# Three side works of a fused attention trunk, moved in its issue order: weight sums, two heads' decay, gate rows

## The chip, the cores and the metric

One core of a Trainium2 chip runs the program. The metric is the device time of one execution in microseconds. A matmul engine (PE, with its weight loads PEld), a vector engine (DVE), a scalar engine (ACT), GpSimd (POOL) and a queue that issues transfers (SP) each work through their own rows in order and meet in semaphores.

## The reference

One layer over 1024 tokens of width 1024. A normalised, modulated input h goes through one wide projection. Its parts feed two gated recurrences, HGRN2 (eight heads) and GLA (four heads), which run chunk by chunk, and their results are projected, gated, merged and projected once more.

```
mod = c_act @ ada_w + ada_b;  shift, scale, gate = split(mod, 3)
h = rms_norm(x, norm_w) * (1 + scale) + shift
hq, hf, hi, hz, gq, gk, gv, gz, ga, mg = split(h @ w_in, IN_OFFSETS)
y_h = hgrn2_branch(hq, hf, hi, hz, ...)                # S_t = diag(f_t) S + k_t v_t^T, o = S^T q
log_a = log_sigmoid(ga @ alpha_w + alpha_b) / 16       # the GLA decay, per head
y_g = gla_branch(gq, gk, gv, gz, log_a, ...)
merged = sigmoid(mg0) * (y_h @ w_branch0) + sigmoid(mg1) * (y_g @ w_branch1)
x = x + gate * (merged @ w_out);  return rms_norm(x, final_norm_w)
```

## The kernel before

**Arithmetic.** Every float32 factor is split in a high part (a cast on ACT, L211) and a low part (a subtraction on DVE, L212), and three matmuls make one product. The large products are cut in 2 x 2 blocks and done as seven block products instead of eight (numbers 1, 2, 5, 3, 6, 7, 4, in this order). Products 5, 3, 6 and 7 need sums of weight blocks, and 5, 6, 7 and 4 need an activation factor of their own.

**Stages.** PE does in turn: a first stage; V0, the GLA values (`Vstage(0)`, L2002); gate and key features of GLA (L607); V1, the HGRN values (`Vstage(1)`, L2002 again); F (`Fstage(2)`), features of HGRN heads; the remaining features (L607); the last stages (L1422) and the output. In the profile V0 runs from 110 to 194 us, the GLA features to 285, V1 to about 375 and F to about 467.

**The stream.** `Stream.go` (L843 on) takes job by job. After every unit, six matmuls or about 1.4 us of PE, it calls `weave`, which steps three tracks: `side` (the attention heads), `more` and `back`. An entry of a track is a generator, a countdown, a rate and the unit from which it may start; only the first entry of a track is stepped, and a generator yields how many units it wants to pass. V0 takes units 0 to 56, the GLA features 56 to 104, V1 104 to 160, F 160 to 216. Before each job, `ahead` loads jobs in advance and prepares (casts and splits) at most the next one, if the pool of 46 slots has room:

```
room = lambda: len(S.free_list)
...
d = self.prepped - i
if d > preps or d > 0 and room() < job.parts + 1:
    break
job.prep()
```

`parts` is 2 for products 1, 2 and 3, whose activation factor lies ready, and 4 for the others. A job that wasn't prepared ahead is prepared when its turn comes. A slot is 128 x 1024 float32; the free slot that was given back first is taken first.

**The side work that the change touches.** `v_sums(s)` (L1819) makes the weight sums of V1 (s = 1) and of F (s = 2). For each half kk it loads four weight blocks (L1829, on SP), makes four sums on DVE (L1832, L1834, L1836, L1838) and stores them from POOL (L1840). `alpha_side((2, 3))` (L932) makes the decay of GLA heads 2 and 3: matmuls (L389), ACT L943 to L960 with several table loads, DVE L949, L950 and L957. `gate_side` (L1086) sums the rows of the gate's modulation on DVE (L1099, L1101). `prepare` (L1280) makes the weight sums of the last stages, with at least 11 free slots, and is held from the start of V1 to near the end of F by `pause`.

**The heads.** `attention` (L639) works a head: ACT L657 and DVE L658 to L661 make a first factor xb from q and the decay, PE scores it (L665), DVE L667 to L670 and L684 scale q and k; DVE L693 and L694 make the next xb for PE L698; DVE L726 and L727 go before PE L767 and L791; DVE L771 and ACT L779 and L795 copy the scores, ACT L792 copies k for PE L815, and DVE L819 and L821 make the state for PE L834 and L836. L1054 loads q and k, L1006 the values; L1019, L1024 and L1030 collect the head's result, and PE L992 and L993, ACT L994 and L995 and DVE L1038 norm it. GLA head 0 runs beside the end of V0 and the first features, head 1 beside the last features, head 2 beside V1. L1888 is DVE's eviction of V0, L1860 ACT's copies out of the accumulator.

The built program has a fixed order of rows on each engine, made by a scheduler from the order in which the code issues them and their dependences, with some rows (`held`) kept in the program's order. Lines behind L1842 are two less in the changed kernel, and the four sums are L1831, L1833, L1835 and L1837 there.

Of the kernel before, what the change touches and what calls it, by code (L numbers as in the profile page):

```python
# [14 lines left out]
ALU = mybir.AluOpType  # L15
# [74 lines left out]
def hybrid_trunk_kernel(  # L90
# [6 lines left out]
    nc = tc.nc  # L97
# [9 lines left out]
    S = Slots(sp, N_SLOTS)  # L107
# [7 lines left out]
    def mtile():  # L115
        cnt[0] += 1
        return ps_m.tile([P, 512], F32, tag="m", name=f"pm{cnt[0]}")
# [79 lines left out]
    def split(src, hi=None, lo=None):  # L197

        if hi is None:
            hi = S.get(list(src.shape[1:]), F32R)  # L200
            lo = S.get(list(src.shape[1:]), F32R)
        nc.scalar.copy(hi, src)  # L202
        nc.vector.tensor_sub(lo, src, hi.bitcast(F32))  # L203
        return hi, lo

    held = tc.keep_in_program_order
# [180 lines left out]
    def mm_alpha(pz, h, sl):  # L387
        for n in range(2):
            nc.tensor.matmul(pz, aw4[:, n, h * P:h * P + P], ga4[:, sl], start=(n == 0), stop=(n == 1))  # L389
# [508 lines left out]
    stream = Stream()  # L898
# [35 lines left out]
    def alpha_side(pair):  # L934
        zs = {}
        while len(S.free_list) < 6:
            yield 1
        for h in pair:
            zb = zs[h] = S.get([T])
            for th in range(2):  # L940
                pz = mtile()
                mm_alpha(pz, h, slice(th * 512, th * 512 + 512))
                nc.scalar.activation(zb[:, th * 512:(th + 1) * 512], pz, AF.Identity,  # L943
                                     bias=vec[:, R_AB + h:R_AB + h + 1])
            yield 2
        S.free(ga4, aw4)
        for h in pair:
            m = alphas[h] = S.get([T])
            nc.vector.tensor_scalar_min(m, zs[h], 0.0)  # L949
            nc.vector.scalar_tensor_tensor(zs[h], m, 2.0, zs[h], ALU.mult, ALU.subtract)  # L950
            yield 2
        for h in pair:
            nc.scalar.activation(zs[h], zs[h], AF.Exp)
        yield 3
        for h in pair:
            nc.scalar.activation(zs[h], zs[h], AF.Ln, bias=one_t)
            nc.vector.tensor_sub(alphas[h], alphas[h], zs[h])  # L957
            yield 2
        for h in pair:
            nc.scalar.activation(alphas[h], alphas[h], AF.Exp, scale=1.0 / TAU)  # L960
            S.free(zs[h])
        yield 3
# [123 lines left out]
    def gate_side():  # L1086

        gacc, gbias = S.get([D]), S.get([D])
        nc.sync.dma_start(gbias[0:1, :], ada_b[0:1, 2 * D:3 * D])
        rows = deque()  # L1090
        for k in range(KT + 2):
            if k < KT:
                b = S.get([D])
                nc.sync.dma_start(b, ada_w[0, k * P:(k + 1) * P, 2 * D:3 * D])
                rows.append(b)
            if k >= 2:
                b = rows.popleft()
                if k == 2:
                    held(nc.vector.tensor_scalar_mul(gacc, b, cs[:, 0:1]))  # L1099
                else:  # L1100
                    held(nc.vector.scalar_tensor_tensor(gacc, b, cs[:, k - 2:k - 1], gacc, ALU.mult, ALU.add))  # L1101
                S.free(b)
            yield 3
        nc.vector.tensor_add(gacc[0:1, :], gacc[0:1, :], gbias[0:1, :])
        hi, lo = split(gacc)
        S.free(gacc, gbias)
        yield 4
        gate_b[0] = S.get([D])
        for half in range(2):
            sl = slice(half * 512, half * 512 + 512)  # L1110
            pg = mtile()
            nc.tensor.matmul(pg, ones_r, hi[:, sl], start=True, stop=False)
            nc.tensor.matmul(pg, ones_r, lo[:, sl], start=False, stop=True)
            nc.scalar.copy(gate_b[0][:, sl], pg)
        S.free(hi, lo)
# [138 lines left out]
    def load_blocks(b, i):  # L1254
        src = sources[b][i]
        x = [S.get([4, 2, P]) for _ in range(2)]
        for kh in range(2):
            nc.sync.dma_start(x[kh].rearrange("p k a f -> p k (a f)"),
                              src[kh * 512:(kh + 1) * 512, :].rearrange("(k p) f -> p k f", p=P))
        return x  # L1260

    def weight_sums(b, i, x1, x2):
        s1, s2 = S.get([2, 4, P]), S.get([2, 4, P])
        parts = {5: s1[:, 0], 6: s1[:, 1], 3: s2[:, 0], 7: s2[:, 1]}
        add = nc.vector.tensor_add
        held(add(parts[7], x1[:, :, 0], x1[:, :, 1]))  # L1266
        yield 1
        held(add(parts[5], x1[:, :, 1], x2[:, :, 1]))
        yield 1
        held(add(parts[6], parts[7], x2[:, :, 1]))  # L1270
        yield 1
        held(add(parts[3], parts[6], x2[:, :, 0]))
        for p, q in SUMS.items():
            nc.gpsimd.dma_start(w_sums[b][i // 2][q][:, i % 2 * 512:i % 2 * 512 + 512],  # L1274
                                parts[p].rearrange("p k f -> p (k f)"))
        S.free(x1, x2)
        S.free(s1, s2, sent=True)
        summed_up.add((b, i))

    def prepare():  # L1280
        todo = [(b, i) for b in range(4) for i in range(4)]
        blocks_of = {}
        for n in range(len(todo) + 1):
            while n < len(todo) and (len(S.free_list) < 11 or paused[0]):
                yield 1
            if n < len(todo):
                blocks_of[n] = load_blocks(*todo[n])
            if n:
                yield from weight_sums(*todo[n - 1], *blocks_of.pop(n - 1))
            yield 5  # L1290
# [466 lines left out]
    for b in (2, 3):  # L1757
        for p, i, z in ((3, 3, "11"), (6, 1, "21"), (6, 3, "12"), (7, 2, "22")):
            after(b - 1, p, i, lambda b=b, z=z: load_quad(b, z))
            if b == 3:  # L1760
                p, i = {(3, 3): (7, 2), (6, 1): (7, 3), (6, 3): (4, 2), (7, 2): (4, 3)}[p, i]
# [27 lines left out]
    vs_d = {s: {p: [dp.tile([P, T], F32, name=f"vs{s}{p}{kk}") for kk in range(2)] for p in SUMS} for s in (1, 2)}  # L1789
# [14 lines left out]
    def load_wq(*at_):  # L1804
        wq[at_] = [S.get([2, 512]) for _ in range(2)]
        for kk in range(2):
            nc.sync.dma_start(wq[at_][kk], w_block(0, *at_, kk)[0][1])
# [11 lines left out]
    def v_sums(s):  # L1819

        add = nc.vector.tensor_add
        for kk in range(2):
            while len(S.free_list) < 9:
                yield 1
            y = {}
            for at_ in ((0, 1), (1, 1), (0, 0), (1, 0)):
                y[at_] = S.get([2, 512])
                for cols, x in w_block(s, *at_, kk):
                    nc.sync.dma_start(y[at_][:, :, cols], x)  # L1829
            yield 8  # L1830
            e = S.get([2, 512])  # L1831
            held(add(e, y[0, 1], y[1, 1]))  # L1832
            yield 2  # L1833
            held(add(y[0, 0], y[0, 0], y[0, 1]))  # L1834
            yield 2  # L1835
            held(add(y[0, 1], y[0, 0], y[1, 1]))  # L1836
            yield 2  # L1837
            held(nc.vector.scalar_tensor_tensor(y[1, 0], y[0, 1], -1.0, y[1, 0], ALU.mult, ALU.subtract))  # L1838
            for p, t in ((5, e), (7, y[0, 0]), (6, y[0, 1]), (3, y[1, 0])):
                nc.gpsimd.dma_start(vs_d[s][p][kk], t.rearrange("p a f -> p (a f)"))  # L1840
            S.free(y[1, 1])
            S.free(e, y[0, 0], y[0, 1], y[1, 0], sent=True)  # L1842
            summed_v.add((s, kk))
            yield 2

# [201 lines left out]
    def front():  # L2047
        alpha = [alpha_half(half) for half in range(2)]
        for i, _ in enumerate(first_group()):
            if i < 10 and i % 2 == 0:  # L2050
                next(alpha[0], None)
            if i == 15:
                for _ in make_ga(1):
                    pass
                load_wq(0, 0)
                load_wq(1, 0)
            elif i in (16, 17, 18, 20, 22):
                next(alpha[1], None)
            elif i == 19:
                stream.ahead(0, 0, 0)  # L2060
        for n, z in enumerate(("12", "22")):
            xq[z] = [hT[1, 2 * n + kk] for kk in range(2)]
        stream.back.append([v_sums(1), 2, 1, 0])
        stream.back.append([v_sums(2), 2, 1, 0])
        stream.back.append([prepare(), 4, 1, 0])
        stream.more.append([alpha_side((2, 3)), 2, 1, 50])
        stream.more.append([gate_side(), 4, 1, 320])

    stream.hooks[2, 0] = begin
    stream.hooks[1, 4] = begin_2  # L2070
    front()
    stream.go()
    S.free(*h_hi, *h_lo)
# [33 lines left out]
```

## Time and profile before

| | |
|---|---|
| median of three runs | 1184.71 us (1183.03 to 1186.02) |
| profiled execution, its own time | 1183.32 us |
| its span | 1181.6 us, mean granted PE clock 0.994 |
| PE busy | 1148.5 us, 97% |
| DVE busy | 842.1 us, 71% |
| ACT busy | 648.5 us, 55% |
| POOL busy | 138.1 us, 12% |
| DMA | 207 GB/s over the span |

The busy shares are means over the whole span. A row of a timeline gives start, duration, engine, line, operation, what it writes and reads, and in brackets how long the engine had stood idle and what ended that. A row of the windows gives the stretch, its length, the busy time of PE, PEld, DVE, ACT and POOL with the count of instructions, the granted PE clock, the share of the DMA engines and GB/s.

### The profile page before, as it was taken

To read this page: it belongs to the slowest core of one execution; us is meant where nothing else is said; L and a number is where in the kernel's file an instruction comes from. 1 tells how busy PE (TensorE), PEld (TensorE's weight loads), DVE (VectorE), ACT (ScalarE), POOL (GpSimd) and SP (SyncE) were. 2 spreads that over 40 slices of the span, in tenths; PEclk is the share of its full clock that TensorE was granted. 3 is DMA by queue.
4 is the path that set the end of the run, shared out by engine and by line. 5 is a ranking of instruction groups with operands and counts; after the bars stand their busy time and mean duration, and the time that the engine had idled before them with its cause. 6 is when DMAs were issued, how large, how long until landed. Compare 5 with 4: busy or idle time off the path is not lost.

```text
span 1181.6 us, 20555 instructions
## 1 busy us (share of the span) xinstructions
PE 1148.5 (97%) x8089; PEld 942.3 (80%) x8089; DVE 842.1 (71%) x1316; ACT 648.5 (55%) x964; POOL 138.1 (12%) x285
## 2 busy tenths in 40 slices
PE   6999999899999999999999999999999999999997
PEld 5777877688888888788888887878888888888886
DVE  4755669657686636987787688695643866988994
ACT  5675455543664758646455445576643644534654
POOL 5121112010011101222211111001110000000000
PEclk8999999999999999999999999999999999999999
DMA  9847369667476546988865674355798846334523
GB/s 319 279 150 245 143 220 306 204 200 259 143 248 197 186 160 188 293 269 276 255 220 178 222 241 137 100 179 173 258 317 288 284 144 225 119 117 161 181 93 137
DMA packets 155986, 245.56 MB, mean 208 GB/s; under 512 B 10139, under 2 KB 107473, under 8 KB 155890
## 3 DMA queue, kind: packets, MB, share of 16 engines
q1 hardware_dynamic: 134866, 174.10, 46.7%
q0 software_dynamic: 20976, 70.15, 15.6%
q8 instruction: 63, 1.03, 0.3%
q14 instruction: 33, 0.27, 0.1%
q10 hardware_dynamic: 48, 0.01, 0.0%
HBM read 170.29 MB, written 73.92 MB: 207 GB/s over the span
## 4 chain that ended last, share of the span: by engine, by line
PE 62%; issue 22%; DVE 5%; POOL 4%; ACT 4%; DMA 2%; SPq 0%; POOLq 0%; ACTq 0%; DVEq 0%
PE pd L1422 14%; PE pd L2002 12%; PE pd L607 9%; PE sc_ps L1422 6%; PE pm L1422 6%; PE pd L1599 3%; PE sc_ps L1599 2%; PE pm L834 2%; POOL ws L1274 2%; PE pm L836 1%; PE pm L1599 1%; PE pm L815 1%; PE pd L396 1%; DMA b<-in_x_dram 1%; POOL v L1867 1%
## 5 line engine op out<-in xcount | busy, mean ns | idle before, releaser
L607 PE MATMUL pd<-b,b 128*128 128x512 f32 x1248 | 301.6, 396 | 0.0
L607 PEld LDWEIGHTS pd<-b,b 128*128 128x128 f32 x1248 | 230.6, 188 | 48.5
L2002 PE MATMUL pd<-b,b 128*128 128x512 f32 x1008 | 237.8, 393 | 4.2 <-DVE b L1888 2.5
L2002 PEld LDWEIGHTS pd<-b,b 128*128 128x128 f32 x1008 | 187.6, 188 | 45.7 <-ACT b L211 2.9
L1422 PE MATMUL pd<-b,b 128*128 128x512 f32 x720 | 169.4, 390 | 0.0
L1422 PEld LDWEIGHTS pd<-b,b 128*128 128x128 f32 x720 | 134.8, 188 | 28.2
L212 DVE TENSOR_TENSOR b<-b,b 128x1024 fp32r<-128x1024 f32 x92 | 110.9, 1222 | 57.1 <-ACT b L211 52.3
L1365 DVE TENSOR_TENSOR b<-b,b 128x1024 fp32r<-128x1024 f32 x56 | 68.2, 1222 | 57.8 <-ACT b L1364 44.7
L211 ACT CAST b<-b 128x1024 fp32r<-128x1024 f32 x92 | 93.3, 1047 | 11.5 <-PE pd L2002 3.8
L1364 ACT CAST b<-b 128x1024 fp32r<-128x1024 f32 x56 | 58.7, 1051 | 63.3 <-PE pm L1422 17.7
L1422 PE MATMUL sc_ps<-b,b 128*128 128x512 f32 x324 | 77.5, 390 | 0.1
L1342 DVE TENSOR_TENSOR b<-b,b 128x1024 fp32r<-128x1024 f32 x48 | 57.9, 1221 | 23.9 <-ACT b L1341 18.7
L1341 ACT CAST b<-b 128x1024 fp32r<-128x1024 f32 x48 | 49.9, 1051 | 41.5 <-PE pd L1422 16.0
L1422 PE MATMUL pm<-b,b 128*128 128x512 f32 x300 | 71.1, 389 | 0.0
L1422 PEld LDWEIGHTS sc_ps<-b,b 128*128 128x128 f32 x324 | 60.6, 188 | 13.0 <-ACT scT L779 0.5
L1422 PEld LDWEIGHTS pm<-b,b 128*128 128x128 f32 x300 | 56.3, 188 | 11.7
L203 DVE TENSOR_TENSOR b<-b,b 128x1024 fp32r<-128x1024 f32 (+1 forms) x37 | 35.7, 976 | 27.5 <-ACT b L202 27.2
L396 PE MATMUL pd<-b,b 128*128 128x512 f32 x192 | 51.9, 403 | 0.9 <-ACT b L202 0.8
L1274 POOL DMA_DIRECT2D ws<-b x64 | 34.5, 540 | 138.2 <-DVE b L1266 52.8
L834 PE MATMUL pm<-scT,b 128*128 128x128 f32 x256 | 47.5, 278 | 2.8 <-DVE b L821 2.6
L726 DVE TENSOR_TENSOR b<-b,tot 128x512 f32<-128x512 f32 x36 | 24.8, 688 | 30.4 <-PE sc_ps L767 29.2
L834 PEld LDWEIGHTS pm<-scT,b 128*128 128x128 f32 x256 | 38.5, 191 | 7.1 <-DVE b L821 4.8
(333 smaller groups left out, 1749.9 us busy)
## 6 DMA issues: line engine op xcount, KB each, us to landing
b<-in_w_in_dram SPq DMA_DIRECT2D x64, 512.0 KB, 6.0
ws<-b POOLq DMA_DIRECT2D x64, 256.0 KB, 5.4
b<-ws SPq DMA_DIRECT2D x32, 512.0 KB, 4.1
b<-in_w_in_dram SPq DMA_DIRECT2D x52, 256.0 KB, 4.0
b<-fx SPq DMA_DIRECT2D x24, 512.0 KB, 4.7
b<-in_x_dram SPq DMA_DIRECT2D x16, 512.0 KB, 6.1
b<-in_ada_w_dram SPq DMA_DIRECT2D x32, 256.0 KB, 6.4
v<-b POOLq DMA_DIRECT2D x32, 256.0 KB, 4.0
```

The source lines that it names most:

```text
L211: held(nc.scalar.copy(hi, src))
L212: nc.vector.tensor_sub(lo, src, hi.bitcast(F32))
L396: nc.tensor.matmul(accs[f], wg(a, d, f), b[d][:, half * 512:half * 512 + 512], start=(d == 0 and n == 0), stop=(d == KT - 1 and n == 2))
L607: nc.tensor.matmul(ps[th][0:w, :], a[:, k, 0:w], b[:, th * 512:(th + 1) * 512], start=(k == 0 and n == 0), stop=(k == KT - 1 and n == 2))
L834: nc.tensor.matmul(o, vch(ch)[:, vh * P:(vh + 1) * P], scT[:, ch, :], start=True, stop=(ch == 0))
L1274: nc.gpsimd.dma_start(w_sums[b][i // 2][q][:, i % 2 * 512:i % 2 * 512 + 512], parts[p].rearrange("p k f -> p (k f)"))
L1342: nc.vector.tensor_sub(lo, src, hi.bitcast(F32))
L1364: nc.scalar.copy(hi, t)
L1365: nc.vector.tensor_sub(lo, t, hi.bitcast(F32))
L1422: nc.tensor.matmul(o, a[:, sl], c, start=(p in (1, 5) and kt == 0 and n == 0), stop=(kt == 3 and n == 2), skip_group_check=True)
L1599: nc.tensor.matmul(o, a, b, start=(p in (1, 5) and kt == 0 and n == 0), stop=(kt == 3 and n == 2), skip_group_check=True)
L2002: nc.tensor.matmul(st.bank[i], l_[:, i * P:(i + 1) * P], r_, start=(p in (1, 5) and kk == 0 and a == 0 and n == 0), stop=(kk == 1 and a == ...
```

## The change

Three things. `v_sums` works in place in four slots instead of five, with the same four sums in another order, the blocks loaded in another order and 8 free slots asked for instead of 9. The track and the start of four side works change: both `v_sums` go from `back` at unit 0 to `more` at unit 56; `gate_side` goes from unit 320 to 300 of `more`, behind them; `alpha_side((2, 3))` goes from `more` at unit 50 to `back` at unit 86; `prepare` follows it in `back` from unit 98.

```diff
-            while len(S.free_list) < 9:
+            while len(S.free_list) < 8:
                 yield 1
             y = {}
-            for at_ in ((0, 1), (1, 1), (0, 0), (1, 0)):
+            for at_ in ((0, 1), (0, 0), (1, 1), (1, 0)):
                 y[at_] = S.get([2, 512])
...
             yield 8
-            e = S.get([2, 512])
-            held(add(e, y[0, 1], y[1, 1]))
-            yield 2
             held(add(y[0, 0], y[0, 0], y[0, 1]))
             yield 2
-            held(add(y[0, 1], y[0, 0], y[1, 1]))
+            held(add(y[0, 1], y[0, 1], y[1, 1]))
             yield 2
-            held(nc.vector.scalar_tensor_tensor(y[1, 0], y[0, 1], -1.0, y[1, 0], ALU.mult, ALU.subtract))
-            for p, t in ((5, e), (7, y[0, 0]), (6, y[0, 1]), (3, y[1, 0])):
-                nc.gpsimd.dma_start(vs_d[s][p][kk], t.rearrange("p a f -> p (a f)"))
-            S.free(y[1, 1])
-            S.free(e, y[0, 0], y[0, 1], y[1, 0], sent=True)
+            held(add(y[1, 1], y[0, 0], y[1, 1]))
+            yield 2
+            held(nc.vector.scalar_tensor_tensor(y[1, 0], y[1, 1], -1.0, y[1, 0], ALU.mult, ALU.subtract))
+            for p, at_ in ((5, (0, 1)), (7, (0, 0)), (6, (1, 1)), (3, (1, 0))):
+                nc.gpsimd.dma_start(vs_d[s][p][kk], y[at_].rearrange("p a f -> p (a f)"))
+            S.free(*y.values(), sent=True)
...
-        stream.back.append([v_sums(1), 2, 1, 0])
-        stream.back.append([v_sums(2), 2, 1, 0])
-        stream.back.append([prepare(), 4, 1, 0])
-        stream.more.append([alpha_side((2, 3)), 2, 1, 50])
-        stream.more.append([gate_side(), 4, 1, 320])
+        stream.more.append([v_sums(1), 1, 1, 56])
+        stream.more.append([v_sums(2), 1, 1, 56])
+        stream.more.append([gate_side(), 4, 1, 300])
+        stream.back.append([alpha_side((2, 3)), 1, 1, 86])
+        stream.back.append([prepare(), 1, 1, 98])
```

How the rows stand now, at two places. The first is SP near the end of V0, where head 0 begins. L589 loads feature weights, L1054 the head's k (`qk4`) and q (`qk0`), L1829 the blocks of `v_sums`, L1006 the head's values. Before:

```order
L589 DMA b154_1566<-in_w_in_dram 128x8x128
L1054 DMA b156_1570<-qk4_697 128x1024
L1829 DMA b157_1578<-in_w_in_dram 128x2x512
L1054 DMA b155_1568<-qk0_693 128x1024
L1829 DMA b158_1580<-in_w_in_dram 128x2x512
L1829 DMA b159_1582<-in_w_in_dram 128x2x512
L1829 DMA b160_1584<-in_w_in_dram 128x2x512
L589 DMA b165_1612<-in_w_in_dram 128x8x128
```

And in the changed kernel:

```order
L589 DMA b154_1566<-in_w_in_dram 128x8x128
L1054 DMA b156_1570<-qk4_697 128x1024
L1054 DMA b155_1568<-qk0_693 128x1024
L589 DMA b161_1604<-in_w_in_dram 128x8x128
L589 DMA b166_1646<-in_w_in_dram 128x8x128
L589 DMA b169_1731<-in_w_in_dram 128x8x128
L1829 DMA b178_1829<-in_w_in_dram 128x2x512
L1829 DMA b176_1825<-in_w_in_dram 128x2x512
```

The four block loads that stood around the load of q stand behind it now, and behind three feature loads.

The second place is V1, while head 1's result is collected and head 2 begins. On DVE, the L212 of `b252` to `b255` are in the kernel before the casts' low parts for product 5's first half (weights and activations):

```order
L212 TENSOR_TENSOR b253_2798<-b236_2652,b252_2797 128x1024
L212 TENSOR_TENSOR b255_2802<-b237_2654,b254_2801 128x1024
L658 TENSOR_TENSOR xb_139<-b260_2853,b182_1794 128x32x8
L1024 SCALAR_TENSOR_TENSOR b217_2317<-pm72_2805,vec_90,b217_2317 128x512
L659 TENSOR_TENSOR xb_139<-b260_2853,b182_1794 128x32x8x2
L667 TENSOR_TENSOR b260_2853<-b260_2853,b182_1794 128x256
L1024 SCALAR_TENSOR_TENSOR b217_2317<-pm73_2816,vec_90,b217_2317 128x512
L1030 TENSOR_TENSOR b250_2763<-b250_2763,b256_2813 128x1024
L660 TENSOR_TENSOR xb_139<-xb_139,b182_1794 128x32x16
L661 TENSOR_TENSOR xb_139<-xb_139,b182_1794 128x32x8
```

In the changed kernel the same two are the L212 of `b255` and `b257`:

```order
L1024 SCALAR_TENSOR_TENSOR b208_2285<-pm73_2797,vec_90,b208_2285 128x512
L1833 TENSOR_TENSOR b232_2651<-b232_2651,b234_2657 128x1024
L1030 TENSOR_TENSOR b246_2751<-b246_2751,b248_2794 128x1024
L1835 TENSOR_TENSOR b234_2657<-b233_2654,b234_2657 128x1024
L658 TENSOR_TENSOR xb_139<-b252_2836,b214_2366 128x32x8
L659 TENSOR_TENSOR xb_139<-b252_2836,b214_2366 128x32x8x2
L667 TENSOR_TENSOR b252_2836<-b252_2836,b214_2366 128x256
L660 TENSOR_TENSOR xb_139<-xb_139,b214_2366 128x32x16
L661 TENSOR_TENSOR xb_139<-xb_139,b214_2366 128x32x8
L669 TENSOR_TENSOR b214_2366<-b214_2366 128x256
L212 TENSOR_TENSOR b255_2849<-b228_2633,b254_2848 128x1024
L212 TENSOR_TENSOR b257_2853<-b229_2635,b256_2852 128x1024
```

They have moved from ahead of head 2's first steps to behind them, and two sums of `v_sums(2)` now lie between head 1's last steps. PE uses them directly behind the last matmul of product 2. Before, six matmuls of product 5 stood there and then head 1's norm:

```order
L2002 MATMUL pd65_1_2659<-b248_2744,b18_155 128x512
L2002 MATMUL pd64_0_2656<-b252_2797,b254_2801 128x512
L2002 MATMUL pd64_0_2656<-b253_2798,b254_2801 128x512
L2002 MATMUL pd64_0_2656<-b252_2797,b255_2802 128x512
L2002 MATMUL pd64_0_2656<-b252_2797,b254_2801 128x512
L2002 MATMUL pd64_0_2656<-b253_2798,b254_2801 128x512
L2002 MATMUL pd64_0_2656<-b252_2797,b255_2802 128x512
L992 MATMUL pm74_2896<-b266_2873,ones_r_85 128x512
L993 MATMUL pm74_2896<-b267_2874,ones_r_85 128x512
```

In the changed kernel head 2's scores stand ahead of product 5:

```order
L2000 MATMUL pd65_1_2640<-b244_2732,b18_155 128x512
L665 MATMUL sc_ps0_72<-xb_139,b218_2466 32x80 x16
L665 MATMUL sc_ps1_73<-xb_139,b218_2466 32x80
L2000 MATMUL pd64_0_2637<-b254_2848,b256_2852 128x512
L2000 MATMUL pd64_1_2638<-b254_2848,b256_2852 128x512
L2000 MATMUL pd65_0_2639<-b254_2848,b256_2852 128x512
L2000 MATMUL pd64_0_2637<-b255_2849,b256_2852 128x512
```

L665 has moved up by 58 rows, to the start of product 5. The norm (L992, L993) stands 26 to 33 rows behind that start instead of 6 to 9.

## The prediction

> **What bounds the kernel now.** I read the page's busy shares first (PE 97%), then the windows of 25 us, since with PE so full only the slices where it is not full can give time back.
>
> ```profile
> 175.00:200.00 25.00, 22.45 (x216) 17.93 (x215) 24.01 (x40) 12.58 (x19) 6.43 (x12) 1.00 0.95 297
> 200.00:225.00 25.00, 19.33 (x185) 15.22 (x184) 15.30 (x26) 17.05 (x26) 1.60 (x3) 0.93 0.67 231
> ...
> 250.00:275.00 25.00, 25.00 (x229) 20.34 (x228) 19.42 (x43) 13.42 (x17) 4.31 (x8) 1.00 0.72 264
> ...
> 325.00:350.00 25.00, 25.00 (x333) 20.27 (x332) 20.84 (x43) 17.37 (x29) 2.14 (x4) 1.00 0.82 270
> ```
>
> The second figure is PE's busy time. Between 175 and 225 us it lacks 8.2 us; in the two later stretches, where attention heads 1 and 2 run, it lacks nothing. PE's timeline names the waits (in brackets: idle time and who ended it):
>
> ```profile
> 178.36 2.98 PE L2002 MATMUL pd<-b,b 128*128 128x512 f32 x12 [2.55 <-DVE b L1888]
> 203.71 0.69 PE L767 MATMUL sc_ps<-b,b 128*64 128x64 f32 x16 [0.76 <-DVE b L727]
> 210.35 0.98 PE L791 MATMUL pm<-ident,b 128*128 128x128 f32 x7 [1.66 <-DVE b L726]
> 217.34 3.07 PE L815 MATMUL pm<-b,b 128*128 128x256 f32 x8 [3.25 <-ACT b L792]
> ```
>
> Together 8.22 us, the whole gap. What stands behind them, in the SP, ACT and DVE timelines:
>
> ```profile
> 162.10 0.38 SPq L1829 DMA_DIRECT2D b<-in_w_in_dram  x1
> 164.43 0.32 SPq L1054 DMA_DIRECT2D b<-qk  x1
> ...
> 173.22 1.05 ACT L657 COPY xb<-b 128x1024 f32<-128x1024 f32 x1 [5.30 <-DMA b<-qk]
> ...
> 208.46 1.23 DVE L957 TENSOR_TENSOR b<-b,b 128x1024 f32<-128x1024 f32 x1 [2.38 <-ACT b L956]
> ...
> 209.39 1.28 ACT L960 ACT_TABLE_LOAD   x1
> 210.69 2.01 ACT L960 ACTIVATE b<-b 128x1024 f32<-128x1024 f32 x2
> ...
> 214.42 1.28 ACT L969 ACT_TABLE_LOAD   x1
> ...
> 216.69 0.98 ACT L792 COPY b<-pm 128x512 f32<-128x512 f32 x2
> ```
>
> Head 0's q load (164.43) is issued behind a weight load of v_sums (L1829), ACT waits 5.30 us for it, and DVE's eviction L1888 queues behind that head's first steps: the 2.55 us. The other three lie among alpha_side's rows (L949 to L960) and v_sums' adds: L957 stalls DVE 2.38 us ahead of the L726 that PE wants, and L792, for which PE waits 3.25 us, stands behind two table loads and both L960. The waits are queueing behind exactly the work that the change takes away from here.
>
> The last of them also cost clock (last column but two):
>
> ```profile
> 215.00:220.00 5.00, 2.67 (x9) 2.23 (x9) 0.91 (x2) 4.12 (x9) 0.00 (x0) 0.81 0.14 55
> 220.00:225.00 5.00, 5.00 (x20) 4.01 (x20) 3.32 (x4) 0.00 (x0) 1.06 (x2) 0.85 0.22 84
> ```
>
> (0.19 + 0.15) x 5 = 1.7 us of full clock, after the 3.25 us wait. The 2.55 us wait left the clock at 1.00 in its window.
>
> **Part 1, head 0 relieved (175 to 225 us).** In the new order both q/k loads of head 0 go out ahead of every L1829, none of alpha_side's rows lies among head 0's on DVE or ACT, and v_sums' first adds come only behind L771. So L1888 no longer queues behind a late head, and L726 and L727 behind no L957. For L792 head 1's ACT rows serve as a scale, where no alpha lies today:
>
> ```profile
> 284.37 2.00 ACT L211 CAST b<-b 128x1024 fp32r<-128x1024 f32 x2
> 286.39 0.97 ACT L792 COPY b<-pm 128x512 f32<-128x512 f32 x2
> ...
> 288.08 1.89 PE L815 MATMUL pm<-b,b 128*128 128x256 f32 x8
> ```
>
> It is ready at 287.36, 0.7 us before PE asks. Head 0 in the new order has no two L211 ahead of it (2.0) but a table load with two L969 (216.69 - 214.42 = 2.3), and two of four L795 move behind it: a margin of 0.5 us or more. So all four waits go: -8.2, and the clock loss with them: -1.7. For new waits behind that thin margin I allow +0.5. Sum -9.4; bounds -9.9 and, if the margin fails by a whole L969 pair, -8.4.
>
> **Part 2, head 1 loaded (250 to 290 us).** Alpha's twelve ACT and DVE steps now lie here. PE's own part of it (L389) is only moved. DVE's is 2 x 0.69 + 2 x 1.22 + 2 x 1.22 = 6.3 us, by the groups of the window 150 to 300:
>
> ```profile
> L957 DVE TENSOR_TENSOR b<-b,b 128x1024 f32<-128x1024 f32 x2 | 2.4, 1222 | 2.4 <-ACT b L956 2.4
> L950 DVE SCALAR_TENSOR_TENSOR b<-b,b 128x1024 f32<-128x1024 f32 x2 | 2.4, 1218 | 0.0
> ...
> L949 DVE TENSOR_SCALAR b<-b 128x1024 f32<-128x1024 f32 x2 | 1.4, 689 | 0.0
> ```
>
> The cover is DVE's idle time and the slack of what PE asks for:
>
> ```profile
> 255.05 1.44 DVE L1038 TENSOR_TENSOR b<-b,b 128x256 f32<-128x256 f32 x4 [8.77 <-ACT b L995]
> ...
> 280.45 0.69 DVE L726 TENSOR_TENSOR b<-b,tot 128x512 f32<-128x512 f32 x1 [2.39 <-PE sc_ps L767]
> ```
>
> One L1831 falls into the 8.77 us; the rest pushes DVE later by about 3 us, of which the 2.39 us before L726 swallow most. About 0.6 us reach L771, L779 and L792, whose slack is the 0.7 us above. Most likely PE waits 0.4 us here (0 to 2.5, the latter if a whole L957 and an L1833 stand ahead of L771 uncovered).
>
> **Part 3, the second value stage (V1) short of slots (315 to 335 us).** v_sums(2) now holds its four slots for its second half at units 105 to 118, just as the stream wants to prepare V1's products one job ahead. That asks for 5 free slots (`job.parts + 1`) when the product has its own factor, and with them taken, the casts of product 5's first half come 4 units (some 5.5 us) later, at its own start. Before, they were early:
>
> ```profile
> 304.42 2.36 DVE L212 TENSOR_TENSOR b<-b,b 128x1024 fp32r<-128x1024 f32 x2 [0.18 <-ACT b L211]
> ...
> 311.26 0.78 DVE L1024 SCALAR_TENSOR_TENSOR b<-pm,vec,b 128x512 f32<-128x512 f32 x1
> 311.92 1.25 DVE L1030 TENSOR_TENSOR b<-b,b 128x1024 f32<-128x1024 f32 x1
> 313.06 0.91 DVE L660 TENSOR_TENSOR xb<-xb,b 128x512 f32<-128x512 f32 x1
> 314.00 0.67 DVE L661 TENSOR_TENSOR xb<-xb,b 128x256 f32<-128x256 f32 x1
> ...
> 310.04 8.46 PE L2002 MATMUL pd<-b,b 128*128 128x512 f32 x36
> 318.35 0.39 PE L992 MATMUL pm<-b,ones_r 128*128 128x512 f32 x1
> ```
>
> PE takes 8.46 / 36 = 0.235 us a matmul, and product 5 begins six matmuls before L992: 318.35 - 1.41 = 316.9. The casts were done at 306.8, ten us ahead. In the new order DVE does, behind the last L1024: L1833, L1030, L1835, the head-2 steps L658, L659, L667, L660, L661, then L669 and only then product 5's two L212. From 311.26 + 0.66, with steps of 1.14 for each of the three large ones (311.92 to 313.06) and 3.2 us for the five small ones (three of L661's 256 elements, two of L660's 512: 3 x 0.67 + 2 x 0.91, less 0.12 overlap each), L661 is done near 318.5. PE's L665 of head 2 has moved up to stand directly ahead of product 5, so PE waits 318.5 - 316.9 = 1.6 us for it, and another 0.6 us for the first low part (two L212 behind L669). Together 2.2.
>
> Then product 3, which head 1's norm (L993 to L995) now meets:
>
> ```profile
> 319.04 0.40 PE L993 MATMUL pm<-b,ones_r 128*128 128x512 f32 x1
> ...
> 322.92 1.06 ACT L995 ACTIVATE b<-b 128x1024 f32<-128x1024 f32 x1
> ...
> 324.01 1.43 DVE L1038 TENSOR_TENSOR b<-b,b 128x256 f32<-128x256 f32 x4 [3.35 <-ACT b L995]
> 325.36 1.22 DVE L212 TENSOR_TENSOR b<-b,b 128x1024 fp32r<-128x1024 f32 x1
> ```
>
> L993 used to stand 42 matmuls ahead of product 3, now 18 (4.2 us). ACT reaches product 3's high cast after L995 (323.98 - 319.04 = 4.9 us after L993), one eviction (0.5) and the cast itself (1.0): 6.5 us, so PE waits 2.3. DVE does its low part behind five L1038 (1.7 us) and a cast of 1.2, 7.9 us after L993; PE by then has three matmuls and an L665: 0.4 more. Sum of part 3: 2.2 + 2.7 = +4.9. Bounds: 0, if evictions or loads shift the heads so that DVE meets the casts in time (nothing here can be a gain, because PE has no wait there today); +9.5, if two more products of V1 wait as product 3 does.
>
> By the Trainium skill (TensorE: Matmul & The Clock Gate, "Part 1: The HAM clock gate"), an idle window of about 3.4 us halves the clock until about as long a busy one has passed, and its section "Why this matters for your kernels" advises to keep gaps under some 3 us. By that rule, and as the two rows on the clock above bear out, the longest wait of part 3 (2.3 us) costs none; one of 3.3 would.
>
> **Part 4, the gate rows 20 units (27 us) earlier.** Seven L1101 and their neighbours, some 12 us of DVE, leave 690 to 725 for 655 to 705:
>
> ```profile
> L1101 DVE SCALAR_TENSOR_TENSOR b<-b,cs,b 128x1024 f32<-128x1024 f32 x7 | 9.0, 1282 | 0.0
> ...
> 675.00:700.00 25.00, 24.20 (x189) 20.18 (x188) 18.89 (x36) 13.04 (x23) 4.27 (x8) 1.00 0.79 268
> 700.00:725.00 25.00, 23.61 (x271) 18.95 (x270) 20.94 (x38) 11.91 (x21) 2.69 (x5) 1.00 0.62 185
> ```
>
> PE lacks 0.8 and 1.4 us in the two windows, so at most 1.4 comes back where the rows leave, and one 1.28 us row in front of a head's step costs about as much: -1.4 to +2, taken as +0.2. DVE has 6.1 us free in the first window, which covers most.
>
> The in-place sums save a slot for each half and no instruction: four adds, four loads and four stores as before. Nothing.
>
> **Sum.** -9.4 + 0.4 + 4.9 + 0.2 = -3.9 us. The profiled execution took 1183.3, 1.4 below the median of the three runs; against the median, 1184.7 - 3.9 = 1180.8 us.
>
> **The rivals.**
> 1. V1 does not stall. If DVE and ACT reach the casts in time (DVE is idle 4.2 us in 325 to 350 already, which speaks for it; the order of rows, which the engines keep, speaks against), parts 1, 2 and 4 are left: -8.8, 1175.9 us.
> 2. The wait in V1 is long enough to lose the clock: the two halves of part 3 with 1 us more on each, 3.3 us at product 3, and 1.7 for the clock as at 217: -3.9 + 2 + 1.7 = -0.2, 1184.5 us. It is the skill's rule at work, told above. For it: a 3.25 us wait did it in this trace. Against: my walk gives 2.3.
> 3. Slower: the shortage of slots carries on through V1. It decides if, after product 3, the remaining halves are still prepared at their own start. Seven halves are left; three with product 3's 2.7 us give +8.1, -3.9 + 8.1 = +4.2, 1188.9 us. For it: each late half frees its slots late for the next. Against: v_sums' slots come back at about unit 118 and it takes none again.
> 4. The gain is not there, because L792 at head 0 still comes late: then 3.25 and the clock's 1.7 stay, +1.0, 1185.7 us. Only alpha's rows stood in front of it, and they are gone.
>
> **How the numbers follow.** Forecast 0.45, rival 1 0.22, rival 2 0.14, rival 3 0.14, rival 4 0.05. A change of 0.3% (3.6 us) is about what a measurement of this kernel can tell from none. The forecast's own range, 1177.5 to 1184, lies for six tenths beyond -3.6: faster 0.27 + 0.22 = 0.49, rounded to 0.5; the rest of it, rival 2 and rival 4 are no change: 0.18 + 0.14 + 0.05 = 0.37, taken as 0.36; slower 0.14. The range for 8 in 10 goes from rival 1 with part 1's upper bound (1175.0) to where rival 3 begins (1187.0).
>
> **What would show it.** Right: no PE wait over 1 us in the profile of after between 170 and 220; a clock of 1.00 there; PE waits of about 2 us each at L665 of head 2 (on L661) and at product 3 (on L211 or L212), some 100 us later; one under 1 us at L815 of head 1. Wrong: PE full from 290 to 340 (rival 1), a clock under 0.9 behind such a wait (rival 2), a third and fourth wait in V1 (rival 3), or L815 of head 0 still waiting (rival 4).

## The result and the profile after

| | before | changed |
|---|---|---|
| median (6 runs each) | 1185.13 us | 1178.40 us |
| lowest to highest | 1183.03 to 1186.02 | 1176.48 to 1180.42 |
| ratio | | 0.9947, 95% interval 0.9932 to 0.9962 |
| profiled execution, its own time | 1183.32 us | 1176.48 us |
| its span, mean granted PE clock | 1181.6 us, 0.994 | 1174.8 us, 0.998 |

The kernel became 6.7 us faster (4.5 to 8.1 by the interval), where the forecast was 3.9; 1178.4 lies in the range. The windows of the changed kernel that answer to those shown of before:

```profile
175.00:200.00 25.00, 25.00 (x333) 20.25 (x332) 19.90 (x45) 7.80 (x16) 3.79 (x7) 1.00 0.98 327
200.00:225.00 25.00, 25.00 (x133) 21.43 (x132) 17.11 (x24) 10.62 (x18) 2.14 (x4) 1.00 0.45 157
...
250.00:275.00 25.00, 25.00 (x336) 20.54 (x335) 24.21 (x45) 18.56 (x28) 2.18 (x5) 1.00 0.91 330
...
300.00:325.00 25.00, 21.23 (x147) 16.18 (x146) 20.44 (x30) 16.74 (x22) 4.84 (x9) 1.00 0.70 237
325.00:350.00 25.00, 25.00 (x278) 20.37 (x277) 22.83 (x43) 18.61 (x33) 2.39 (x5) 1.00 0.81 269
```

The hole between 175 and 225 is closed and the clock there is whole. A new hole of 3.8 us stands at 300 to 325, in V1. Of the stretches shown DVE is now busiest in head 1's, 24.2 of 25 us, without a PE wait in it. Head 0's rows on SP, ACT and PE:

```profile
160.22 3.79 SPq L1054 DMA_DIRECT2D b<-qk  x2
164.21 8.59 SPq L589 DMA_DIRECT2D b<-in_w_in_dram  x3
173.54 0.40 SPq L1829 DMA_DIRECT2D b<-in_w_in_dram  x1
...
201.31 1.28 ACT L969 ACT_TABLE_LOAD   x1
...
203.58 0.97 ACT L792 COPY b<-pm 128x512 f32<-128x512 f32 x2
...
205.90 1.89 PE L815 MATMUL pm<-b,b 128*128 128x256 f32 x8
```

Both loads of head 0 go out ahead of the weight sums' first block, and L792 is done at 204.55, 1.35 us before PE's L815, which has no bracket any more. The PE waits of over 0.15 us between 150 and 460 us, all of them:

```profile
277.34 1.99 PE L815 MATMUL pm<-b,b 128*128 128x256 f32 x8 [0.46 <-ACT b L792]
307.91 0.85 PE L665 MATMUL sc_ps<-xb,b 128*32 128x80 f32 x34 [1.39 <-ACT b L211]
323.57 0.51 PE L2000 MATMUL pd<-b,b 128*128 128x512 f32 x1 [2.38 <-ACT b L211]
358.41 0.70 PE L815 MATMUL pm<-b,b 128*128 128x256 f32 x2 [0.18 <-DVE b L821]
```

These are the places that the prediction named: head 1's L815 (0.4 forecast), head 2's L665 (1.6), product 3 (2.3). The rows behind the last two, on DVE and ACT:

```profile
301.00 1.22 DVE L1833 TENSOR_TENSOR b<-b,b 128x1024 f32<-128x1024 f32 x1
302.13 1.22 DVE L1030 TENSOR_TENSOR b<-b,b 128x1024 f32<-128x1024 f32 x1
303.27 1.22 DVE L1835 TENSOR_TENSOR b<-b,b 128x1024 f32<-128x1024 f32 x1
304.41 0.65 DVE L658 TENSOR_TENSOR xb<-b,b 128x256 f32<-128x256 f32 x1
...
307.12 0.64 DVE L661 TENSOR_TENSOR xb<-xb,b 128x256 f32<-128x256 f32 x1
...
321.04 1.06 ACT L995 ACTIVATE b<-b 128x1024 f32<-128x1024 f32 x1
322.01 0.57 ACT L1858 COPY b<-pd 128x512 f32<-128x512 f32 x1
322.47 1.05 ACT L211 CAST b<-b 128x1024 fp32r<-128x1024 f32 x1
```

L661 ends at 307.76 and PE's L665 starts at 307.91; product 3's cast ends at 323.52 and PE starts at 323.57. The profile puts the first wait down to a cast that ended at the same moment (307.78). The prediction had a second term at each of the last two places, 0.6 us more behind L665 and 0.4 us more behind product 3's cast; neither came as a wait.

Where the time went, by the first row of each stage in PE's timeline (us; the last two columns are used below):

| stage | before | changed | difference | forecast | gate from 320 | sums from 50 |
|---|---|---|---|---|---|---|
| start to first stage's products | 21.67 | 20.92 | -0.75 | 0 | 21.52 | 22.14 |
| first stage | 88.30 | 88.29 | 0.0 | 0 | 88.26 | 88.25 |
| V0 | 83.56 | 78.94 | -4.6 | -9.4 with the next | 78.95 | 78.94 |
| GLA features | 91.70 | 85.73 | -6.0 | | 85.72 | 85.71 |
| V1 and F | 199.34 | 205.15 | +5.8 | +5.3 | 206.65 | 199.21 |
| remaining features | 298.25 | 296.88 | -1.4 | +0.2 | 298.43 | 297.17 |
| last stages | 316.06 | 316.14 | +0.1 | 0 | 316.75 | 316.14 |

V0 loses 2.5 us of wait and the eight L389, which go over to the next stage. The start isn't touched by the change; it lies between 20.5 and 22.3 us in the profiled executions of all the kernels here, so its 0.75 us is chance. V1 and F by windows, before and then in the changed kernel:

```profile
285.23:484.57 199.34, 197.62 (x1468) 164.82 (x1466) 130.53 (x207) 129.06 (x184) 20.45 (x38) 1.00 0.62 201
273.88:479.03 205.15, 199.16 (x1467) 164.48 (x1465) 135.29 (x212) 130.37 (x186) 22.95 (x43) 1.00 0.62 205
```

PE's idle time there grew from 1.7 to 6.0 us, short gaps included, which is 4.3 of the 5.8 us. The other 1.5 us are longer busy time of the same matmuls, at a clock of 1.00.

### The profile page after: what moved, and what is told of

Same layout as the page of the kernel before. It is cut to its first block, busy times and chain, and to the rows that moved or that the text cites. A ratio compares the mean times of both kernels' runs of the same rounds, so it can differ in the third digit from the quotient of the medians.

```text
span 1174.8 us, 20553 instructions
## 1 busy us (share of the span) xinstructions
PE 1148.9 (98%) x8089; PEld 942.3 (80%) x8089; DVE 842.1 (72%) x1316; ACT 646.8 (55%) x963; POOL 138.3 (12%) x285
## 4 chain that ended last, share of the span: by engine, by line
PE 76%; DVE 8%; ACT 7%; DMA 4%; issue 3%; SPq 1%; DVEq 0%; ACTq 0%
PE pd L2000 16%; PE pd L607 15%; PE pd L1422 14%; PE sc_ps L1422 6%; PE pm L1422 6%; PE pd L1599 3%; DMA b<-in_ada_w_dram 2%; PE pd L396 2%; PE pm L834 2%; DMA b<-in_w_in_dram 2%; PE sc_ps L1599 2%; PE pm L836 2%; PE pm L1599 1%; ACT b L211 1%; PE pm L815 1%
## 5 line engine op out<-in xcount | busy, mean ns | idle before, releaser
L607 PEld LDWEIGHTS pd<-b,b 128*128 128x128 f32 x1248 | 230.0, 188 | 48.2
L2000 PEld LDWEIGHTS pd<-b,b 128*128 128x128 f32 x1008 | 187.4, 188 | 45.8 <-ACT b L211 2.8
L1422 PEld LDWEIGHTS pd<-b,b 128*128 128x128 f32 x720 | 134.8, 188 | 28.3
L212 DVE TENSOR_TENSOR b<-b,b 128x1024 fp32r<-128x1024 f32 x92 | 110.7, 1221 | 55.0 <-ACT b L211 53.5
L396 PEld LDWEIGHTS pd<-b,b 128*128 128x128 f32 x192 | 34.3, 188 | 11.9 <-ACT b L202 1.8
```

What stands on the lines that cost most here:

```text
L396: nc.tensor.matmul(accs[f], wg(a, d, f), b[d][:, half * 512:half * 512 + 512], start=(d == 0 and n == 0), stop=(d == KT - 1 and n == 2))
L607: nc.tensor.matmul(ps[th][0:w, :], a[:, k, 0:w], b[:, th * 512:(th + 1) * 512], start=(k == 0 and n == 0), stop=(k == KT - 1 and n == 2))
L1422: nc.tensor.matmul(o, a[:, sl], c, start=(p in (1, 5) and kt == 0 and n == 0), stop=(kt == 3 and n == 2), skip_group_check=True)
L2000: nc.tensor.matmul(st.bank[i], l_[:, i * P:(i + 1) * P], r_, start=(p in (1, 5) and kk == 0 and a == 0 and n == 0), stop=(kk == 1 and a == ...
```

## The experiments

The kernel before ran again beside the experiments, with medians of 1183.05, 1182.72 and 1183.58 us (22, 15 and 9 runs) instead of 1185.13. Each ratio below is to the runs taken with it; the changed kernel's 1178.40 is not from these series, so a difference to it is known to some 2 us only.

**Theory A**: V1 waits because the weight sums for F hold four slots at units 105 to 118, so that V1's product 5 is cast at its own start, and head 1's norm and product 3 slide together behind it. **Theory B**: it is the sums' own work on DVE, next to head 1's last steps. **Theory C**: the 1.4 us in the remaining features come from the gate rows.

**1. Sums six units earlier.**

```diff
-        stream.more.append([v_sums(1), 1, 1, 56])
-        stream.more.append([v_sums(2), 1, 1, 56])
+        stream.more.append([v_sums(1), 1, 1, 50])
+        stream.more.append([v_sums(2), 1, 1, 50])
```

> The changed kernel with both weight sums started at unit 50 instead of 56, nothing else. In its order of rows V1's product 5 is cast in advance again (the casts stand ahead of head 2's first steps) and head 1's norm stands 42 matmuls ahead of product 3, while the four sums still lie beside the end of head 1. Theory A (V1 waits because the sums hold slots at units 105 to 118, so that product 5 is prepared at its own start): the waits of 1.4 us at L665 and 2.4 us at product 3 go, time 4 to 5 us under the changed kernel, about 1174. Theory B (it is the sums' work on DVE beside head 1's last steps that is late, the slots don't matter): the waits stay, within 1 us of the changed kernel, 1178.

Measured: 1172.02 us (1171.54 to 1172.06), ratio to before 0.9903 (0.9888 to 0.9918). V1 in its profile, on PE:

```profile
299.85 8.46 PE L2000 MATMUL pd<-b,b 128*128 128x512 f32 x36
308.15 0.39 PE L992 MATMUL pm<-b,ones_r 128*128 128x512 f32 x1
...
309.08 11.05 PE L2000 MATMUL pd<-b,b 128*128 128x512 f32 x48
320.06 1.31 PE L665 MATMUL sc_ps<-xb,b 128*32 128x80 f32 x64
```

No bracket is left, the norm stands six matmuls into product 5 as before the change, and V1 and F take 199.21 us, what they took before. The sums' adds still lie beside head 1 (an L1837 between two L1024, at 293.95). The median is 6.4 us under the changed kernel, where 4 to 5 were expected; V1 and F alone give 5.9 in the profile. That speaks for A and against B, although the adds no longer stand between the last L1024 and L1030.

**2. Sums held longer, their adds out of the way.**

```diff
-            yield 8
+            yield 20 if (s, kk) == (2, 1) else 8
```

> The changed kernel, where the last half of v_sums(2) waits 20 units instead of 8 between its loads and its sums: the slots stay taken longer, and the sums L1833 and L1835 no longer stand between head 1's last steps and head 2's first. Theory A: product 5 is still prepared at its own start, so product 3's wait of about 2.4 us stays; the wait at L665 shrinks by the 2.3 us of the two sums, to 0 or 0.3; time 1 to 2 us under the changed kernel, 1177. Theory B: both waits go, 1174.

Measured: 1179.66 us (1176.89 to 1181.17), ratio to before 0.9964 (0.9952 to 0.9976). Both waits stay, 2.24 at product 3 as theory A had it, and 1.52 at L665, against it. On DVE and PE:

```profile
302.07 1.22 DVE L1030 TENSOR_TENSOR b<-b,b 128x1024 f32<-128x1024 f32 x1
305.55 0.67 DVE L658 TENSOR_TENSOR xb<-b,b 128x256 f32<-128x256 f32 x1 [2.26 <-DMA b<-qk]
...
309.11 0.99 PE L665 MATMUL sc_ps<-xb,b 128*32 128x80 f32 x42 [1.52 <-ACT b L211]
...
324.99 0.50 PE L2000 MATMUL pd<-b,b 128*128 128x512 f32 x1 [2.24 <-ACT b L211]
```

With the two adds gone, DVE stands 2.26 us for head 2's load of q, and L658 starts as late as with them. In the changed kernel the load (issued at 301.09, and ACT's L657, which needs it, starts at 304.34) and the adds (L1835 ends at 304.49) end together, and the prediction saw only the adds. What made L665 wait is its place in the order, directly behind product 2; each of the two alone is late for that place. Theory B falls: without the adds, both waits are there. The time expected was 1177; the clock that this profile lost behind product 3 is in the last section.

**3. The shortage alone, in the kernel before.**

```diff
+    vjobs[1][4].parts = 24
```

Only the test for free slots reads this number; product 5's first half is then never prepared in advance.

> The kernel before, where only V1's product 5, first half, asks for so many free slots that it is never prepared in advance; nothing else is changed. Theory A in its plain form (preparing at its own start is enough for a wait): new PE waits of 2 to 4 us in V1, time 1187 to 1189. Theory A with its condition (the late casts cost only where head 1's norm is pushed behind them; here it keeps its place ahead of product 5, as the order of rows has it): under 1 us, 1185 to 1186. Theory B: no new wait, 1185.

Measured: 1184.07 us (1180.55 to 1185.80), ratio 1.0005 (0.9993 to 1.0016): no change. In its profile product 5 waits 0.40 us:

```profile
314.64 0.39 PE L993 MATMUL pm<-b,ones_r 128*128 128x512 f32 x1
314.96 1.31 PE L665 MATMUL sc_ps<-xb,b 128*32 128x80 f32 x64
316.67 5.51 PE L2002 MATMUL pd<-b,b 128*128 128x512 f32 x23 [0.40 <-ACT b L211]
```

So late casts alone cost next to nothing. Here the norm stands ahead of product 5 and its table loads run under product 5's 48 matmuls. Theory A holds only with its condition: it is the norm behind product 5, close ahead of product 3, that costs. No run moves the norm alone, so the condition is inferred from this kernel against the changed one.

**4. Gate rows back at 320.**

```diff
-        stream.more.append([gate_side(), 4, 1, 300])
+        stream.more.append([gate_side(), 4, 1, 320])
```

> The changed kernel with the gate rows started at unit 320 again, as before. The trace of the changed kernel gains about 1.4 us between 690 and 830 us against the one of before. Theory C (that gain is the gate rows' move): the PE waits at L815 and L834 between 690 and 760 come back, time 1 to 2 us over the changed kernel, about 1180. Rival: it is chance, the same time as the changed kernel, 1178.4 with less than 0.7 between.

Measured: 1180.16 us (1177.95 to 1182.41), ratio to before 0.9974 (0.9962 to 0.9985). The stage of the remaining features takes 298.43 us, as before the change (298.25), against 296.88. The waits of PE between 640 and 835 us, with their total, count and longest, of this kernel:

```profile
PE pm L834 <- DVE b L821: 2.5, 4, 1.1
PE pm L815 <- ACT b L792: 2.0, 3, 1.5
```

and of the changed kernel:

```profile
PE pm L834 <- DVE b L821: 1.2, 2, 0.6
PE pm L815 <- ACT b L792: 0.8, 3, 0.4
```

That is 4.5 us of wait against 2.4 (with 0.4 at an L698 in the changed kernel). Theory C stands for the stage in the profile; the whole kernels are 1.8 us apart, and their intervals touch.

**5. The decay alone.** In the kernel before:

```diff
         stream.back.append([v_sums(2), 2, 1, 0])
-        stream.back.append([prepare(), 4, 1, 0])
-        stream.more.append([alpha_side((2, 3)), 2, 1, 50])
+        stream.back.append([alpha_side((2, 3)), 1, 1, 86])
+        stream.back.append([prepare(), 1, 1, 98])
```

> The kernel before with alpha_side alone moved to unit 86 (and prepare behind it at 98); weight sums at unit 0 and gate rows at 320 as before. If the parts add: the waits at L791 and L815 of head 0 and their clock loss go (1.7 + 3.3 + up to 1.7 us), the 2.55 us at L1888 behind the load of q stays, V1 keeps its advance casts and waits under 0.5 us; time 1177 to 1178.5, 5 to 7 us under the kernel before. Rival: the sums' adds fill head 0's gap by themselves, the waits at L791 and L815 stay in part, 1181 or more.

Measured: 1182.04 us (1178.98 to 1184.95), ratio 0.9992 (0.9979 to 1.0004): no change that can be told, and not what was expected. V0 took 2.1 us less (L389 went out of it) and the GLA features 7.9 less, but V1 and F 206.85 us instead of 199.34:

```profile
302.82 1.23 DVE L957 TENSOR_TENSOR b<-b,b 128x1024 f32<-128x1024 f32 x1 [1.05 <-ACT b L956]
...
310.82 1.66 PE L2002 MATMUL pd<-b,b 128*128 128x512 f32 x6 [1.49 <-ACT b L1860]
317.44 1.10 PE L993 MATMUL pm<-b,ones_r 128*128 128x512 f32 x2 [1.97 <-DVE b L203]
```

A track steps only its first entry, and here the old weight sums stand ahead of alpha_side until V1. So alpha's rows run in V1 (L957 at 302.8), and the norm is late for another reason. The start unit of an entry is a lower bound, and I had read it as the time.

**6. The sums alone.**

```diff
+        stream.more.append([alpha_side((2, 3)), 2, 1, 50])
         stream.more.append([v_sums(1), 1, 1, 56])
         stream.more.append([v_sums(2), 1, 1, 56])
-        stream.more.append([gate_side(), 4, 1, 300])
-        stream.back.append([alpha_side((2, 3)), 1, 1, 86])
+        stream.more.append([gate_side(), 4, 1, 320])
```

> The changed kernel with alpha_side back at unit 50 of its old track, ahead of the weight sums, and the gate rows at 320: the sums' move alone. If the parts add: the 2.55 us behind the load of q go, head 0's waits by alpha's rows (4 to 5 us and the clock) stay, and V1's shortage stands as in the changed kernel or worse, since the sums start behind alpha: 4 to 7 us lost there. Time 1184 to 1188, no better than the kernel before. Rival: the sums' move carries the gain, 1179.

Measured: 1190.11 us (1188.18 to 1191.86), ratio 1.0069 (1.0054 to 1.0084). It is slower than before, by more than was expected:

```profile
202.22 0.46 PE L762 MATMUL sc_ps<-xb 128*32 128x32 f32 x32 [2.79 <-ACT xb L718]
...
314.14 1.27 PE L665 MATMUL sc_ps<-xb,b 128*32 128x80 f32 x58 [2.54 <-DVE xb L661]
334.08 19.38 PE L2000 MATMUL pd<-b,b 128*128 128x512 f32 x72 [5.12 <-ACT b L211]
```

Head 0 still waits behind alpha's rows, and the sums, which start behind alpha, fall deeper into V1. The last of the sums' adds lies at 357 us, against 316 in the changed kernel. Neither half of the change gains by itself, as built here (experiment 5 did not put alpha's rows where the change puts them); together they do, because each frees the other's place.

**7. Sums for F from unit 124**, behind V1's first product 5, the others as in the change.

```diff
-        stream.more.append([v_sums(2), 1, 1, 56])
+        stream.more.append([v_sums(2), 1, 1, 124])
```

> The changed kernel with v_sums(1) at 56 and v_sums(2) only from unit 124, behind V1's first product 5: the slots are free at units 105 to 118, the sums for F are made beside V1's second half. Theory A: the two waits in V1 go as with unit 50; time 1172 to 1173.5, up to 1 us more if the sums meet head 2. Rival (the sums are late for F and their products wait on the load): 1176 or more.

Measured: 1174.41 us (1172.86 to 1174.45), ratio to before 0.9927 (0.9915 to 0.9940). The two waits are gone a second way, and the norm stands six matmuls into product 5 again; one wait of 1.07 us stands at 346.7, and V1 and F take 200.55 us.

**8. to 10. Nearer to the best unit.** The sums at 50 with the gate rows at 280 and at 260, and the sums at 47 with the gate rows at 280; the first of them:

```diff
-        stream.more.append([v_sums(1), 1, 1, 56])
-        stream.more.append([v_sums(2), 1, 1, 56])
-        stream.more.append([gate_side(), 4, 1, 300])
+        stream.more.append([v_sums(1), 1, 1, 50])
+        stream.more.append([v_sums(2), 1, 1, 50])
+        stream.more.append([gate_side(), 4, 1, 280])
```

> The weight sums from unit 50 and the gate rows from 280 instead of 300. Theory C, that the gate rows cost only where DVE is already full: 0 to 1 us under the same kernel with 300 (1172.0). Rival: they now fall among another head's steps and cost 0.5 to 1.5 us, 1173.

> The weight sums from unit 50 and the gate rows from 260. Gate rows at 320, 300 and 280 gave 298.4, 296.9 to 297.2 and 295.9 us for the stage from F's end to the last stages. Theory C (they cost where DVE is full, and DVE has more room the earlier they come): 0 to 1 us under 280, about 1170. Rival: with 280 nothing of theirs is left to save, 1170 to 1171 and the stage again at 296.

> The weight sums from unit 47 and the gate rows from 280. If unit 50 stands safely inside the region where slots are free in time, 47 gives the same, 1170 to 1171. If the block loads now come ahead of head 0's steps again and make DVE late at L1888, a wait of 1 us or more returns near 175 us and the time is 1171.5 or more.

Measured: 1170.28 us (1170.01 to 1171.08), ratio to before 0.9897 (0.9884 to 0.9911), for 50 and 280; 1174.09 (1173.64 to 1174.29) for 50 and 260; 1180.24 (1178.76 to 1180.57) for 47 and 280. The first is 1.7 us under the sums at 50 with the gate rows at 300, more than the 0 to 1 expected. The remaining features take 295.94 us with the gate at 280 and 298.69 at 260 (297.17 at 300), where PE waits at another head and at the gate rows' own matmul:

```profile
600.34 1.31 PE L665 MATMUL sc_ps<-xb,b 128*32 128x80 f32 x64 [1.41 <-DVE xb L661]
627.15 0.50 PE L1112 MATMUL pm<-b,ones_r 128*128 128x512 f32 x1 [0.95 <-ACT b L792]
```

At 260 two L1101 (593.63 and 597.76) stand on DVE between that head's L660 and L661. So "earlier is better" is wrong for theory C: the gate rows cost where they meet a head's steps. PE's listed waits in the stage are 3.9 us at 280 and 6.3 at 260. With the sums at 47 it isn't L1888 that waits, as I feared, but L815 of head 0, in the ACT and PE timelines:

```profile
209.42 1.04 ACT L657 COPY xb<-b 128x1024 f32<-128x1024 f32 x1 [9.38 <-DMA b<-qk]
210.49 0.74 ACT L779 COPY scT<-sc_ps 64x256 f32<-64x256 f32 x2
...
214.17 3.78 PE L815 MATMUL pm<-b,b 128*128 128x256 f32 x8 [6.80 <-ACT b L792]
```

Head 1's first copy now stands ahead of head 0's L779 on ACT and waits there 9.4 us for its own load. Three units decide on 10 us. The version with 50 and 280 beats both kernels.

## Why the prediction was right, point by point

- **Part 1** (-9.4): right in every step. The four waits and the clock loss went, L792 has 1.35 us where 0.5 or more was worked out. V0 and the GLA features together lost 10.6 us; 8.2 of wait and 1.7 of clock leave 0.7, which is not wait: it lies in PE's busy time (167.04 against 164.67 us, the 1.7 of clock in it). Which matmuls it comes from stays open.
- **Part 2** (+0.4): 0.46 us, at the row named.
- **Part 3** (+4.9): 1.4 + 2.4 = 3.8 us of wait, against 2.2 + 2.7; the stage lost 5.8 with part 2, and the other 1.5 us lies in PE's own busy time, not in gaps, as the windows above show. The slots as the cause are shown by experiments 1 and 7, where the sums give them back earlier or take them later, and 2, where they keep them and only the adds have moved; the condition of experiment 3 is added to that. That the stage's total comes near the forecast (+5.8 against +5.3) is in part luck: two terms did not come, and 1.5 us came that the prediction did not have. One reason in it was incomplete: L665 was late by the adds and just as late by its load of q (experiment 2).
- **Part 4** (+0.2): wrong in sign and size, -1.4 (experiment 4). The step that failed set the price of one L1101 ahead of a head's step against what comes back where the rows leave. The return came (L815's longest wait there, 1.6 us, fell to 0.4) and no such price did: PE's listed waits in the stage fell from 6.0 to 4.6 us.
- **Rival 2**, the clock: in the profile of the changed kernel nothing was lost, but the same waits did lose clock in the profiles of experiments 2 and 4, as the last section shows. So the statement that a 2.3 us wait costs none is wrong for some executions.
- **Rivals 1, 3 and 4** did not happen. V1 stalled, but not on and on: behind product 3 one wait of 0.18 us is listed.
- **The size**: the sum was -3.9; the median moved by -6.7, by 4.5 at the least within the interval. The profiles explain the difference by part 4 (-1.6 against the forecast), part 1 (-1.2), the start (-0.75), which is chance, and parts 2 and 3 (+0.5).

## What to carry to other kernels

When a side work moves, look at the resource that it holds while it waits, and not only at its instructions: here four slots held for 13 units undid the advance preparation of a job and cost about half of the gain, and starting the same work six units earlier gave it back. A start time in a queue of generators is only a bound, so single parts of such a change do not add up; each place must be walked in the order of rows that the whole change makes. And a row that moves up to the place directly behind a long stretch of matmuls becomes late by whatever is last there, so removing one cause uncovers the next.

## What the runs showed of the hardware

PE's granted clock falls in steps of one size, and on a grid. Here are windows of 3.41 us, laid so that one begins where the clock falls. First the decay alone:

```profile
314.18:317.59 3.41, 1.44 (x7) 0.90 (x6) 3.41 (x4) 2.60 (x4) 0.38 (x1) 1.00 1.01 348
317.59:321.01 3.42, 3.42 (x9) 2.66 (x10) 2.96 (x4) 3.38 (x5) 0.16 (x1) 0.50 0.81 272
...
720.37:723.78 3.41, 1.61 (x11) 1.15 (x10) 1.72 (x3) 3.40 (x7) 0.00 (x0) 1.00 0.17 65
723.78:727.19 3.41, 3.41 (x15) 3.02 (x14) 3.41 (x8) 3.06 (x7) 0.00 (x0) 0.50 0.00 0
```

PE is idle for 3.41 - 1.44 = 1.97 us of the first window and for 1.80 us of the third. The window behind each runs at half the clock, which loses 3.41 x 0.5 = 1.7 us, and the two falls lie 119 windows apart. Experiment 2 shows the same with 2.24 us idle:

```profile
322.60:326.01 3.41, 1.17 (x25) 0.66 (x24) 2.46 (x6) 3.41 (x6) 1.07 (x2) 1.00 0.49 159
326.01:329.42 3.41, 3.41 (x11) 2.73 (x9) 3.41 (x6) 2.73 (x3) 1.60 (x4) 0.50 0.89 309
```

In the same way 2.42 us idle from 321.37 on in the kernel with the gate at 320, and 2.65 from 214.68 on in the kernel before, lose 1.7 us each. Behind the longest waits on record, 5.12 us (experiment 6) and 6.80 us (the sums at 47), two windows in a row ran at half the clock. The kernel of experiment 3 loses nothing behind a longer wait, of 3.27 us, that ends at 215.93 (the windows are counted on from the end of the low clock at its start, 19.74):

```profile
210.88:214.30 3.42, 1.78 (x8) 1.13 (x6) 1.23 (x1) 3.36 (x5) 0.54 (x1) 1.00 0.98 319
214.30:217.71 3.41, 1.78 (x9) 1.60 (x9) 0.58 (x2) 3.36 (x8) 0.00 (x0) 1.00 0.03 12
217.71:221.12 3.41, 3.41 (x16) 2.82 (x16) 3.23 (x5) 0.05 (x1) 0.53 (x1) 1.00 0.00 0
```

A border of the grid cuts this wait in two, 1.64 and 1.63 us. The changed kernel's 2.38 us are cut the same way, 1.48 us with 0.90 behind the border. In the profiles of all twelve kernels, behind the first 25 us, every full-clock window with 1.80 us of idle PE or more (eight of them) is followed by one at half the clock, and none with 1.67 or less is. So a wait of 1.8 to 3.3 us costs either nothing or 1.7 us, by where the grid happens to cut it in that execution; in these profiles the idle time inside one window decided, not the length of the wait.

The Trainium skill (TensorE: Matmul & The Clock Gate, "Part 1: The HAM clock gate") describes a gate that halves the clock after an idle window of about 3.4 us, and windows that run freely of the program. The half clock and the grid of 3.41 us agree with it, but here 1.80 us idle within a window were enough. Its advice ("Why this matters for your kernels") to keep gaps under some 3 us is not enough here: waits of 1.80 and 1.97 us were hit.

Where the grid cuts a wait would also explain how far the times of one kernel lie apart: the kernel before with its 3.25 us wait and the changed one with 2.38 us spread over 3.0 and 3.9 us in six runs each, the sums at 50, with no wait over 1 us behind the first 25 us, over 0.5 in four. No experiment tried this, but the clocks on record go with it: of 22 runs of the kernel before in one series, the five with a mean clock of 0.990 or 0.991 took 1183.95 to 1186.33 us, the three with 0.997 took 1181.18 to 1182.92.
